# A hybrid decoder trunk on one core: both parts of the input in one 512-column matmul in layer 1

## The chip, the cores and the metric

The kernel runs on one core of a Trainium2 chip. The time is the device time of one execution in microseconds; lower is better. The core has five engines that work side by side and meet through semaphores: PE (TensorE, the matrix multiplier; its weight loads are shown apart as PEld), DVE (VectorE), ACT (ScalarE), POOL (GpSimd) and SP (SyncE, which issues the transfers from the chip's memory). Each engine takes its instructions in the order in which the program wrote them. Matmul results go to PSUM, a memory of eight banks of 512 float32 per partition, and are read from there by ACT or DVE; everything else lies in SBUF.

## The reference

A decoder trunk of two layers, one sequence of 256 tokens behind 16 learned meta tokens, width 2048, all in float32. Layer 0 mixes by attention and a short convolution, layer 1 by a state-space layer (S5) with a gated linear unit behind it; a feed-forward network (FFN) with 5632 hidden channels follows in each.

```python
def s5_mixer(u, ...):
    ...
    g = jax.nn.gelu(y).astype(u.dtype)
    return (g @ w_glu1) * jax.nn.sigmoid(g @ w_glu2)

def swiglu_ffn(h, w_gate, w_up, w_down):
    return (jax.nn.silu(h @ w_gate) * (h @ w_up)) @ w_down

def reference(...):
    h = jnp.concatenate([meta, x], axis=1)
    for i in range(DEPTH):
        u = rms_norm(h, norm_g[i, 0])
        m = attn_conv_mixer(u, ...) if i % 2 == 0 else s5_mixer(u, ...)
        h = h + rms_norm(m, norm_g[i, 1])
        f = swiglu_ffn(rms_norm(h, norm_g[i, 2]), ffn_w_gate[i], ffn_w_up[i], ffn_w_down[i])
        h = h + rms_norm(f, norm_g[i, 3])
    return h[:, N_META:]
```

The change touches `g @ w_glu1`, `g @ w_glu2`, and the products with `w_gate` and `w_up` of layer 1.

## The kernel before

Channels lie on partitions and tokens in the free dimension: an activation is 16 tiles of 128 channels x 272 tokens, in layer 1 from the GLU on 256 (the meta tokens are dropped). A float32 product is made of three matmuls in a faster type (float32r): the weights and the input are each split into a first part and a rest, and hi x xh, hi x xl and lo x xh are added up in PSUM (`mm3`; the fourth product is left out). `xh` and `xl` are the input's parts, `whi` and `wlo` those of the weights.

```python
    def mm3(ps, hi, lo, bh, bl, first, last):
        nc.tensor.matmul(ps, hi, bh, start=first, stop=False)
        nc.tensor.matmul(ps, hi, bl, start=False, stop=False)
        nc.tensor.matmul(ps, lo, bh, start=False, stop=last)
```

Weights come in chunks of two input tiles by up to three output tiles (`Weights`). A chunk is fetched by a DMA issued on SP (`raw`, four buffers), cast on ACT to `whi` (L101), and `raw - whi` is written on DVE as `wlo` (L108). `W.next()`, called ahead of each chunk's matmuls, writes into the program the cast for the chunk two further on and the subtraction for the next one. As the order of an engine is the order of writing, these splits stand on ACT and DVE among whatever else the program writes there at that place. `tick()`, called behind each chunk, writes one piece of queued side work.

The GLU (L1301 on) goes over six blocks of three or two output tiles, 16 chunks each: the second product's and the first's, by turns. After the second product's last chunk (the 14th of the block) ACT takes tanh of each output tile straight from PSUM (L1328); after the first product's last chunk (the 16th) `gate` multiplies on DVE (`tt`, L812) and squares on ACT for the norm. In the first and the last block the gates stand right there, in the others they are queued over the next chunks.

The FFN (`ffn`) goes over thirds of the hidden channels, five blocks of three output tiles each (the very last has two), each block with 16 chunks: gate and up by turns for c = 0 to 7. For c = 0 the matmuls go by part instead of by tile (L755), for c = 1 to 7 `mm3` is called. I number a block's chunks 0 to 15, so 14 is the gate's last and 15 the up's last; 16 and 17 are the first two of what follows. In the last chunks each output tile is multiplied by the norm's factor on DVE on its way out of PSUM (L764 to `gs`, L766 to `us`), and after the gate tiles ACT takes one tanh of all three (L768). Four queued steps then make the hidden activation and its two parts (L774 to L776). A third ends with the down projection, in layer 1 `last_down` (L1379 to L1381), whose moving operand is the weights, 512 columns wide. The first block of each FFN also runs `Sandwich`, which makes the input tiles as the block needs them. A block holds six of the eight PSUM banks, one per output tile and product, of which 256 of 512 columns are used in layer 1.

## Time and profile before

| | us |
|---|---|
| three runs | 2413.26, 2414.88, 2415.72 |
| median | 2414.88 |
| span of the profiled execution (its first to its last instruction) | 2412.0 |

For the profiled execution the span is what is given; it lies 2.9 us under the median of the runs. Of this span the state-space layer ends and the GLU begins at about 1452 us, the GLU ends at 1642, layer 1's FFN runs from there to the end: gate and up blocks to 1826, the first down projection to 1912, and so on by thirds.

In the lines of the profile "L285" is line 285 of the kernel before; `mm<-xh,whi` names what is written and what is read; a shape such as 128x256 is partitions by columns; times in timelines and chains are the start and the length in us, counted from the span's start. A name behind "<-" in square brackets or behind a bar is what ended the idle time before the instruction.

### The profile page before, as it was taken

The page shows a single profiled execution, that of the slowest core. Times are in us where ns is not written, and L with a number is a line of the kernel's source. Part 1 is how long each engine was busy: PE and PEld are TensorE (multiplying, and loading weights), DVE is VectorE, ACT ScalarE, POOL GpSimd, SP SyncE. Part 2 cuts the span into 40 slices and gives each one's busy share as a digit, 9 for nine tenths or more (in the row PEclk, how much of TensorE's full clock was granted, in tenths as well). Part 3 has the DMA queues.
Part 4 walks back from the last instruction along what each step waited for, and adds up shares of the span by engine and source line. Part 5 has one row for each costly group of instructions (what it writes and reads, how often), then busy time and mean ns, then how long its engine had stood idle before and what let it go on. Part 6 is the DMA issues. An engine that isn't in the chain of part 4 may idle for free.

```text
span 2412.0 us, 45528 instructions
## 1 busy us (share of the span) xinstructions
PE 2364.2 (98%) x18038; PEld 2272.2 (94%) x18038; DVE 1437.0 (60%) x2004; ACT 1060.0 (44%) x1613; POOL 705.3 (29%) x1221
## 2 busy tenths in 40 slices
PE   8999999999999999999999889999999999999998
PEld 7999999999999999999999779998998899989996
DVE  6555555686754665656654796457655455645665
ACT  5434434463444343434444555445444444433443
POOL 3000000148775778568501452105000000000001
PEclk9999999999999999999999889999999999999999
DMA  6555555456776777776755864555666566656654
GB/s 171 135 152 142 151 134 181 131 172 182 227 215 208 215 208 215 219 202 200 224 184 166 272 218 157 185 170 155 193 187 206 179 182 179 201 184 186 189 189 155
DMA packets 392537, 447.35 MB, mean 185 GB/s; under 512 B 75476, under 2 KB 324084, under 8 KB 392180
## 3 DMA queue, kind: packets, MB, share of 16 engines
q1 hardware_dynamic: 392096, 444.37, 62.1%
q8 instruction: 141, 2.31, 0.4%
q14 instruction: 72, 0.59, 0.1%
q10 hardware_dynamic: 228, 0.08, 0.0%
HBM read 413.50 MB, written 30.87 MB: 184 GB/s over the span
## 4 chain that ended last, share of the span: by engine, by line
PE 89%; DVE 7%; ACT 1%; DMA 1%; issue 1%; POOL 1%; DVEq 0%; ACTq 0%; SPq 0%; POOLq 0%
PE mm L285 23%; PE mm L287 23%; PE mm L286 23%; PE mm L755 5%; PE mm L1381 3%; PE mm L1380 3%; PE mm L1379 3%; DVE wlo L108 1%; DVE v L1172 1%; DMA raw<-in_ffn_w_gate_dram 1%; PE mm L1030 1%; PE mm L1018 1%; PE aux L483 0%; DVE m L812 0%; DVE rc L812 0%
## 5 line engine op out<-in xcount | busy, mean ns | idle before, releaser
L108 DVE TENSOR_TENSOR wlo<-raw,whi 128x768 fp32r<-128x768 f32 (+2 forms) x891 | 939.7, 1066 | 508.2 <-ACT whi L101 503.7
L101 ACT CAST whi<-raw 128x768 fp32r<-128x768 f32 (+2 forms) x891 | 776.2, 884 | 797.7 <-PE mm L286 496.2
L285 PE MATMUL mm<-xh,whi 128*128 128x272 f32 (+1 forms) x3744 | 1078.0, 288 | 1.0 <-DVE m L812 0.6
L287 PE MATMUL mm<-xh,wlo 128*128 128x272 f32 (+1 forms) x3744 | 1072.8, 287 | 2.7 <-DVE wlo L108 2.1
L286 PE MATMUL mm<-xl,whi 128*128 128x272 f32 (+1 forms) x3744 | 1066.6, 285 | 2.2 <-DVE xl L719 2.1
L287 PEld LDWEIGHTS mm<-xh,wlo 128*128 128x128 f32 x3744 | 707.0, 189 | 6.2 <-DVE wlo L108 6.2
L285 PEld LDWEIGHTS mm<-xh,whi 128*128 128x128 f32 x3744 | 708.6, 189 | 3.6 <-ACT sq L297 0.8
L286 PEld LDWEIGHTS mm<-xl,whi 128*128 128x128 f32 x3744 | 707.3, 189 | 3.2 <-DVE xl L719 3.2
L285 PE MATMUL mm<-ah,whi 128*128 128x272 f32 x960 | 277.6, 289 | 0.5 <-ACT m L678 0.5
L287 PE MATMUL mm<-ah,wlo 128*128 128x272 f32 x960 | 277.0, 289 | 0.0
L286 PE MATMUL mm<-al,whi 128*128 128x272 f32 x960 | 275.7, 287 | 0.0
L812 POOL TENSOR_TENSOR m<-m,gb 128x512 f32<-128x512 f32 x8 | 12.1, 1509 | 711.5 <-ACT mm L1393 695.0
L285 PEld LDWEIGHTS mm<-ah,whi 128*128 128x128 f32 x960 | 180.8, 188 | 1.1 <-ACT m L678 0.7
L286 PEld LDWEIGHTS mm<-al,whi 128*128 128x128 f32 x960 | 180.6, 188 | 0.0
L287 PEld LDWEIGHTS mm<-ah,wlo 128*128 128x128 f32 x960 | 180.3, 188 | 0.1
L302 POOL TENSOR_TENSOR sqacc<-sqacc,sq 128x272 f32<-128x272 f32 (+1 forms) x81 | 83.8, 1035 | 242.9 <-ACT sq L297 241.1
L1380 PE MATMUL mm<-wlo,ah 128*128 128x512 f32 x352 | 137.8, 392 | 1.0 <-DVE wlo L108 1.0
L1379 PE MATMUL mm<-whi,ah 128*128 128x512 f32 x352 | 138.6, 394 | 0.0
L1381 PE MATMUL mm<-whi,al 128*128 128x512 f32 x352 | 138.3, 393 | 0.0
L764 DVE TENSOR_TENSOR gs<-mm,r 128x272 f32<-128x272 f32 (+1 forms) x88 | 38.1, 433 | 113.1 <-PE mm L287 113.1
L580 POOL TENSOR_TENSOR z<-c,x 128x272 f32<-128x272 f32 x8 | 6.3, 792 | 302.7 <-DVE x L573 201.2
L1380 PEld LDWEIGHTS mm<-wlo,ah 128*128 128x128 f32 x352 | 66.2, 188 | 16.3 <-DVE wlo L108 1.7
(408 smaller groups left out, 2509.8 us busy)
## 6 DMA issues: line engine op xcount, KB each, us to landing
raw<-in_ffn_w_gate_dram SPq DMA_DIRECT2D x224, 384.0 KB, 3.8
raw<-in_ffn_w_up_dram SPq DMA_DIRECT2D x224, 384.0 KB, 3.8
raw<-in_ffn_w_down_dram SPq DMA_DIRECT2D x168, 512.0 KB, 4.5
raw<-in_ab_w_in_dram SPq DMA_DIRECT2D x90, 512.0 KB, 4.0
raw<-in_s_w_glu_dram SPq DMA_DIRECT2D x64, 384.0 KB, 3.6
raw<-in_ab_w_o_dram SPq DMA_DIRECT2D x32, 512.0 KB, 4.3
w<-scr SPq DMA_DIRECT2D x16, 768.0 KB, 4.3
scr<-xw SPq DMA_DIRECT2D x16, 512.0 KB, 4.6
```

Source lines behind the costliest of these rows:

```text
L101: self.nc.scalar.copy(hi[:, :n], self.raw[i][:, :n])
L108: self.nc.vector.tensor_tensor(lo[:, :n], raw[:, :n], hi[:, :n].bitcast(F32), op=ALU.subtract)
L285: nc.tensor.matmul(ps, hi, bh, start=first, stop=False)
L286: nc.tensor.matmul(ps, hi, bl, start=False, stop=False)
L287: nc.tensor.matmul(ps, lo, bh, start=False, stop=last)
L302: eng.tensor_tensor(self.acc[:, :self.cols], self.acc[:, :self.cols], sq[:, :self.cols], op=ALU.add)
L755: nc.tensor.matmul(pss[o], w[:, k, o * P:(o + 1) * P], xx[:, k, :cols], start=(k == 0 and w is hi and xx is xh), stop=False)
L764: nc.vector.tensor_tensor(gs[:, o, :cols], pss[o], r["r"][:, :cols], op=ALU.mult)
L1018: nc.tensor.transpose(pt[:, j * P:(j + 1) * P], wide["b"][:, i, j].rearrange("p s h -> p (s h)"), ident)
L1379: nc.tensor.matmul(pss[a], ah[:, kt, ts_], hi[:, k], start=(kt == 0), stop=False)
L1380: nc.tensor.matmul(pss[a], ah[:, kt, ts_], lo[:, k], start=False, stop=False)
L1381: nc.tensor.matmul(pss[a], al[:, kt, ts_], hi[:, k], start=False, stop=(kt == kts - 1))
```

## The change

`xh` and `xl` become the two halves of one tile `xx`, so that one access pattern holds both parts of an input tile. In layer 1's GLU and in layer 1's FFN for c = 1 to 7, `mm2` passes both parts by the same `whi` in one matmul of 512 columns: hi x xh goes to the first half of a PSUM bank and hi x xl to the second; lo x xh then adds to the first half. For c = 0 of the FFN three matmuls remain, of which the one with xl writes the second half. The halves are added later by `both`: ACT copies the second half to SBUF, DVE adds the first. As the norm's factor or the gate no longer comes in the same instruction, POOL multiplies by it in SBUF. In the GLU the second product's tiles are copied, added, and then go through tanh. Layer 0 and the down projections stay.

```diff
-    xh = keep.tile([P, KT, NT], F32R, name="xh")
-    xl = keep.tile([P, KT, NT], F32R, name="xl")
+    xx = keep.tile([P, 2, KT, NT], F32R, name="xx")
+    xh, xl = xx[:, 0], xx[:, 1]
...
+    def mm2(ps, hi, lo, kt):
+        nc.tensor.matmul(ps, hi, xx[:, :, kt, :NREAL], start=(kt == 0), stop=False, skip_group_check=True)
+        nc.tensor.matmul(ps[:, :NREAL], lo, xx[:, 0, kt, :NREAL], start=False, stop=(kt == KT - 1), skip_group_check=True)
+
+    def both(out, ps):
+        nc.scalar.copy(out, ps[:, NREAL:])
+        nc.vector.tensor_tensor(out, out, ps[:, :NREAL], op=ALU.add)
...
     def ffn(m, sw, cols, down=None):
...
-                gps = [bank()[:, :cols] for _ in range(n)]
-                ups = [bank()[:, :cols] for _ in range(n)]
+                halves = cols == NREAL
+                wide_ = 2 * cols if halves else cols
+                gps = [bank()[:, :wide_] for _ in range(n)]
+                ups = [bank()[:, :wide_] for _ in range(n)]
...
                         if c == 0:
                             for k in range(2):
-                                for w, xx in ((hi, xh), (lo, xh), (hi, xl)):
+                                for w, xp in ((hi, xh), (lo, xh), (hi, xl)):
+                                    at = cols if halves and xp is xl else 0
                                     for o in range(n):
-                                        nc.tensor.matmul(pss[o], w[:, k, o * P:(o + 1) * P], xx[:, k, :cols], start=(k == 0 and w is hi and xx is xh), stop=False)
+                                        nc.tensor.matmul(pss[o][:, at:at + cols], w[:, k, o * P:(o + 1) * P], xp[:, k, :cols],
+                                                         start=(k == 0 and w is hi and xp is xh), stop=False, skip_group_check=halves)
...
                         for o in range(n):
                             for k in range(2):
                                 kt = 2 * c + k
-                                mm3(pss[o], hi[:, k, o * P:(o + 1) * P], lo[:, k, o * P:(o + 1) * P],
-                                    xh[:, kt, :cols], xl[:, kt, :cols], False, kt == KT - 1)
-                            if c == 7 and pss is gps:
-                                nc.vector.tensor_tensor(gs[:, o, :cols], pss[o], r["r"][:, :cols], op=ALU.mult)
-                            elif c == 7:
-                                nc.vector.tensor_tensor(us[:, o, :cols], pss[o], r["h"][:, :cols], op=ALU.mult)
+                                w = hi[:, k, o * P:(o + 1) * P], lo[:, k, o * P:(o + 1) * P]
+                                if halves:
+                                    mm2(pss[o], *w, kt)
+                                else:
+                                    mm3(pss[o], *w, xh[:, kt, :cols], xl[:, kt, :cols], False, kt == KT - 1)
+                            if c == 7:
+                                d, rr = (gs, r["r"]) if pss is gps else (us, r["h"])
+                                d, rr = d[:, o, :cols], rr[:, :cols]
+                                if halves:
+                                    both(d, pss[o])
+                                    nc.gpsimd.tensor_tensor(d, d, rr, op=ALU.mult)
+                                else:
+                                    nc.vector.tensor_tensor(d, pss[o], rr, op=ALU.mult)
...
     for a, b in GLU_BLOCKS:
...
         def gate(o, a=a, p1=p1):
-            tt(mr[:, a + o], p1[o], ths[a][:, o], M_)
-            osq.add(mr[:, a + o])
+            t = mr[:, a + o]
+            both(t, p1[o])
+            tt(t, t, ths[a][:, o], M_, G)
+            osq.add(t)
...
-                    mm3((p2, p1)[i][o], hi[:, k, o * P:(o + 1) * P], lo[:, k, o * P:(o + 1) * P],
-                        xh[:, kt, :NREAL], xl[:, kt, :NREAL], kt == 0, kt == KT - 1)
+                    mm2((p2, p1)[i][o], hi[:, k, o * P:(o + 1) * P], lo[:, k, o * P:(o + 1) * P], kt)
...
                 for o in range(n):
-                    nc.scalar.activation(th[:, o], p2[o], AF.Tanh, scale=0.5)
+                    both(th[:, o], p2[o])
+                    nc.scalar.activation(th[:, o], th[:, o], AF.Tanh, scale=0.5)
```

Where a block of layer 1's FFN ends, ACT's rows before are these (first block of the second third; the numbers in names are the weights' chunks, 687 being the next block's first, 688 its second; what an instruction waits for is the engine named in its brackets, DMAHW a transfer):

```order
L101 CAST whi687_22941<-raw687_22873 128x768 [waits DMAHW5_49,DVE_49,PE_49]
L768 ACTIVATE th_22604<-gs_22602 128x3x256 [waits DVE_49]
L101 CAST whi688_22969<-raw688_22897 128x768 [waits DMAHW6_49,PE_49,Activation_49]
L101 CAST whi689_23005<-raw689_22921 128x768 [waits DMAHW7_49,PE_49,Activation_49]
L101 CAST whi690_23030<-raw690_22945 128x768 [waits DMAHW0_49,PE_49,Activation_49]
```

and in the changed kernel

```order
L101 CAST whi687_22060<-raw687_22010 128x768 [waits DMAHW5_49,DVE_49,PE_49]
L297 COPY gs_21793<-mm_21787 128x256 [waits PE_49]
L297 COPY gs_21793<-mm_21788 128x256 [waits PE_49]
L297 COPY gs_21793<-mm_21789 128x256 [waits PE_49]
L790 ACTIVATE th_21795<-gs_21793 128x3x256 [waits Pool_49]
L101 CAST whi688_22088<-raw688_22028 128x768 [waits DMAHW6_49,DVE_49]
L297 COPY us_21794<-mm_21790 128x256 [waits PE_49]
L297 COPY us_21794<-mm_21791 128x256 [waits PE_49]
L297 COPY us_21794<-mm_21792 128x256 [waits PE_49]
L101 CAST whi689_22124<-raw689_22046 128x768 [waits DMAHW7_49,DVE_49]
```

Six copies stand among the casts, and the tanh waits for POOL instead of DVE. DVE's rows at the same place before:

```order
L764 TENSOR_TENSOR gs_22602<-mm_22598,r_20305 128x256 [waits PE_49]
L108 TENSOR_TENSOR wlo687_22971<-raw687_22873,whi687_22941 128x768 [waits DMAHW5_49,Activation_49]
L766 TENSOR_TENSOR us_22603<-mm_22599,rh_20308 128x256 [waits PE_49]
L766 TENSOR_TENSOR us_22603<-mm_22600,rh_20308 128x256 [waits PE_49]
L766 TENSOR_TENSOR us_22603<-mm_22601,rh_20308 128x256 [waits PE_49]
L108 TENSOR_TENSOR wlo688_23007<-raw688_22897,whi688_22969 128x768 [waits DMAHW6_49,DVE_49,Activation_49]
L774 SCALAR_TENSOR_TENSOR gs_22602<-th_22604,gs_22602 128x3x256 [waits DVE_49]
```

and now

```order
L298 TENSOR_TENSOR gs_21793<-gs_21793,mm_21789 128x256 [waits Activation_49]
L108 TENSOR_TENSOR wlo687_22090<-raw687_22010,whi687_22060 128x768 [waits DMAHW5_49,DVE_49]
L298 TENSOR_TENSOR us_21794<-us_21794,mm_21790 128x256 [waits Activation_49]
L298 TENSOR_TENSOR us_21794<-us_21794,mm_21791 128x256 [waits Activation_49]
L298 TENSOR_TENSOR us_21794<-us_21794,mm_21792 128x256 [waits Activation_49]
L108 TENSOR_TENSOR wlo688_22126<-raw688_22028,whi688_22088 128x768 [waits DMAHW6_49,DVE_49]
L796 SCALAR_TENSOR_TENSOR gs_21793<-th_21795,gs_21793 128x3x256 [waits Pool_49]
```

The places on DVE are the same; the multiplies that waited for PE are adds that wait for ACT's copies, and the gate product waits for POOL. In the GLU, after the second product's last chunk of the second block, ACT before had these rows (chunk numbers 494 to 497, 494 being that block's last):

```order
L101 CAST whi494_18280<-raw494_18212 128x768 [waits DMAHW3_49,DVE_49,PE_49]
L1328 ACTIVATE th_18304<-mm_17962 128x256 [waits PE_49]
L1328 ACTIVATE th_18304<-mm_17963 128x256 [waits PE_49]
L1328 ACTIVATE th_18304<-mm_17964 128x256 [waits PE_49]
L101 CAST whi495_18308<-raw495_18236 128x768 [waits DMAHW4_49,DVE_49]
```

and now

```order
L101 CAST whi494_18117<-raw494_18067 128x768 [waits DMAHW3_49,DVE_49,PE_49]
L297 COPY th_18135<-mm_17877 128x256 [waits PE_49]
L1352 ACTIVATE th_18135<-th_18135 128x256 [waits DVE_49]
L297 COPY th_18135<-mm_17878 128x256 [waits PE_49]
L1352 ACTIVATE th_18135<-th_18135 128x256 [waits DVE_49]
L297 COPY th_18135<-mm_17879 128x256 [waits PE_49]
L1352 ACTIVATE th_18135<-th_18135 128x256 [waits DVE_49]
L101 CAST whi495_18145<-raw495_18085 128x768 [waits DMAHW4_49,Activation_49]
```

Between one tile's copy and its tanh ACT now waits for an add on DVE, three times in a row, ahead of the next cast.

More of the change, by code (lines that the diff above doesn't have):

```diff
@@ L1302, in trunk @@
         n = b - a
-        p2 = [bank()[:, :NREAL] for _ in range(n)]
-        p1 = [bank()[:, :NREAL] for _ in range(n)]
+        p2 = [bank() for _ in range(n)]
+        p1 = [bank() for _ in range(n)]
         now = a == 0 or b == KT
```

## The prediction

> **What bounds the kernel now.** I read the page's busy line and chain first, then stretches of layer 1, then the chain and the timeline inside one stretch. On the page TensorE is busy all the time and is most of the chain:
>
> ```profile
> span 2412.0 us, 45528 instructions
> PE 2364.2 (98%) x18038; PEld 2272.2 (94%) x18038; DVE 1437.0 (60%) x2004; ACT 1060.0 (44%) x1613; POOL 705.3 (29%) x1221
> PE 89%; DVE 7%; ACT 1%; DMA 1%; issue 1%; POOL 1%; DVEq 0%; ACTq 0%; SPq 0%; POOLq 0%
> ```
>
> The windows of layer 1 (start:end, length, busy time and count of PE, PEld, DVE, ACT, POOL, granted clock, DMA share, GB/s) are the gated linear unit (GLU) behind its first block, the first block of the FFN, the next four blocks, and the first down projection:
>
> ```profile
> 1490.00:1640.00 150.00, 149.39 (x1258) 149.22 (x1257) 76.04 (x99) 68.19 (x108) 13.30 (x14) 1.00 0.56 181
> 1640.00:1684.00 44.00, 40.06 (x297) 37.68 (x295) 37.46 (x54) 27.83 (x55) 31.33 (x29) 0.92 0.47 137
> 1684.00:1822.00 138.00, 137.37 (x1161) 137.40 (x1162) 79.40 (x102) 60.84 (x76) 0.00 (x0) 1.00 0.64 191
> 1826.00:1908.00 82.00, 82.00 (x376) 67.42 (x375) 39.09 (x37) 38.30 (x48) 0.00 (x0) 1.00 0.62 199
> ```
>
> PE bounds all but the first FFN block, where DVE is the fuller engine (37.46 of 44). In the FFN's blocks POOL does nothing at all. A block's own price comes from the chain (start, length), a 512-column matmul's from the timeline of PE, first and last of 14 rows:
>
> ```profile
> 604.77 4.53 PE mm L755 x36
> 1689.56 4.27 PE mm L755 x36
> ...
> 1723.65 4.27 PE mm L755 x36
> ```
>
> ```profile
> 1889.82 0.39 PE L1379 MATMUL mm<-whi,ah 128*128 128x512 f32 x1
> ...
> 1892.80 0.39 PE L1380 MATMUL mm<-wlo,ah 128*128 128x512 f32 x1
> ```
>
> A block of 288 matmuls of 256 columns takes 1723.65 - 1689.56 = 34.09 us without a gap: 118.4 ns each. Thirteen steps of 512 columns take 2.98 us: 229.2 ns each.
>
> **What it saves.** For each output tile and input tile, three matmuls of 256 columns (355.2 ns) become one of 512 and one of 256 (229.2 + 118.4 = 347.6): 7.6 ns less. The columns streamed stay the same; only one matmul's fixed part goes. There are 16 x 2 x 16 = 512 such triples in the GLU and 44 x 2 x 14 = 1232 in the FFN (its first chunk of each pass keeps three). The first FFN block's 84 give nothing, since DVE sets its pace. 1660 x 7.6 ns = 12.6 us. Bounds, as no row shows two halves 17 KB apart as one moving operand: nothing, if the two halves cost what two matmuls do; and 11.4 ns (18.9 us), if a 256-column matmul behind a 512-column one pays its columns alone (229.2 / 2 = 114.6). I take the rows as they are.
>
> [...]
>
> That fewer weight loads free PE is in the same price: at 272 columns 36 matmuls took 4.53 us against 4.27, so columns, not loads, set the step, and the 512-column rows already hide their load. DMA moves the same bytes. Merging the two parts into one tile changes nothing in layer 0, whose instructions keep their order and waits.
>
> **What it adds.** Each output tile was read out of PSUM by one DVE multiply. Now ACT copies the second half, DVE adds the first, and POOL multiplies (FFN 88 times, GLU gates 16); the GLU's tanh inputs take copy, add, tanh. That is 120 ACT, 16 DVE and 104 POOL instructions more. Their sum is nothing against the idle shares above. What counts is where they stand: ACT and DVE run in order, and behind them stand the weight splits for which PE waits. Here is the end of an FFN block before, chunk 15 (up, c = 7) starting at T = 1755.47, chunk 16 and 17 being the next block's first gate and up chunk:
>
> ```profile
> 1755.35 0.28 PE L287 MATMUL mm<-xh,wlo 128*128 128x256 f32 x1
> 1755.47 0.28 PE L285 MATMUL mm<-xh,whi 128*128 128x256 f32 x1
> ...
> 1759.70 0.53 PE L755 MATMUL mm<-xh,whi 128*128 128x256 f32 x3
> 1760.07 0.52 PE L755 MATMUL mm<-xh,wlo 128*128 128x256 f32 x3
> ```
>
> ```profile
> 1755.67 0.42 DVE L764 TENSOR_TENSOR gs<-mm,r 128x256 f32<-128x256 f32 x1 [0.29 <-PE mm L287]
> 1756.01 0.95 DVE L108 TENSOR_TENSOR wlo<-raw,whi 128x768 fp32r<-128x768 f32 x1
> ...
> 1758.12 0.95 DVE L108 TENSOR_TENSOR wlo<-raw,whi 128x768 fp32r<-128x768 f32 x1
> ```
>
> ```profile
> 1756.12 0.85 ACT L768 ACTIVATE th<-gs 128x768 f32<-128x768 f32 x1 [4.03 <-DVE gs L764]
> 1756.88 2.29 ACT L101 CAST whi<-raw 128x768 fp32r<-128x768 f32 x3
> ```
>
> The second row of wlo is chunk 17's, done at T+3.60; PE asks for it at T+4.60. It has 1.0 us to spare. Prices for the new work (one line's min/median/max ns, then a group with its mean), and from the first FFN block how POOL and DVE fare side by side:
>
> ```profile
> L678 ACT COPY m<-mm x28: 367/385/387, 396.4 to 776.2; 128x272 f32<-128x272 f32 x28
> L1207 POOL TENSOR_TENSOR yq<-yq,yy x16: 723/922/1447, 1375.1 to 1475.7; 128x256 f32<-128x256 f32 x16
> ```
>
> ```profile
> L680 DVE TENSOR_TENSOR m<-m,mm 128x272 f32<-128x272 f32 x32 | 13.3, 437 | 40.0 <-PE mm L287 40.0
> ```
>
> ```profile
> 1656.54 2.90 DVE L108 TENSOR_TENSOR wlo<-raw,whi 128x768 fp32r<-128x768 f32 x2
> 1657.17 1.45 POOL L711 TENSOR_TENSOR hT<-hT,hn 128x256 f32<-128x256 f32 x1
> 1658.59 1.44 POOL L302 TENSOR_TENSOR sqacc<-sqacc,sq 128x256 f32<-128x256 f32 x1
> ```
>
> Alone, a wlo split is 0.95 and a POOL multiply 0.72; side by side both take 1.45. After the change, with 0.03 us per hand-over (1756.09 to 1756.12):
> - gate tiles leave PE at T-1.19, T-0.49 and T+0.20; each is copied (0.38) and added (0.44), and POOL takes them one after the other: from T-0.33, T+0.40 and T+1.13, the last beside chunk 16's wlo (1.4) until T+2.5.
> - tanh, which waits for POOL, starts at T+2.56 and not T+0.65. Behind it on ACT stand chunk 17's whi (0.76 later) and then the three copies of the up tiles (0.76 after that, 0.35 apart): the third ends at T+5.16, its add at T+5.6.
> - chunk 17's wlo stands behind those adds on DVE, beside POOL's up multiplies: T+5.6 + 1.45 = T+7.0.
> - PE asks for it at 2.09 + 2.13 + 0.36 = T+4.58: it waits 2.4 us. Chunk 18's wlo, behind the gate product on DVE (1.4), ends at T+9.3 where PE asks at T+9.1: 0.2 more. Chunk 19's is in time, and the splits catch up at 0.9 us of DVE for 2.1 of PE.
>
> So 2.6 us at each block's end. Where a third ends and the down projection follows, chunk 17 is asked for 0.6 us later, but cast and split are longer: about the same. Fourteen blocks of three tiles x 2.6 + 1.5 for the last of two = 37.9 us. Bounds: without any meeting of POOL and DVE (multiply 0.72, split 0.95) the third up copy ends at T+4.5 and the split at T+5.85: 1.3 us each, 19 in all. If each op shuts the other out for its whole length, splits and multiplies take turns, chunk 17's comes at T+6.9 and chunk 18's at T+10.2: 3.7 each, 54 in all. I take the middle, since the rows show sharing.
>
> In the GLU the second product's tiles go copy, add, tanh three times in a row on ACT, each turn 0.38 + 0.44 + 0.38 and hand-overs, 1.26 us. Counted from chunk 14's start the third add ends at 2.2, chunk 15's wlo behind it at 3.0, and PE asks at 2.3: 0.7 x 6 blocks = 4.2. The first block gates at once, and each gate's square on ACT waits for POOL: a turn of 2.05, the third add at 3.8, chunk 17's wlo at 4.7 against 2.3: 2.4. At the GLU's end nothing covers it:
>
> ```profile
> 1641.48 1.28 ACT L381 ACT_TABLE_LOAD   x1
> 1642.77 0.20 ACT L381 ACTIVATE warm_t<-eps_t 128x1 f32<-128x1 f32 x1
> 1642.88 0.70 ACT L297 ACTIVATE sq<-m 128x256 f32<-128x256 f32 x2
> 1643.33 0.61 PE L314 MATMUL mm<-mean_w,sq 128*128 128x1 f32 x4 [0.91 <-ACT sq L297]
> ```
>
> Two turns of 2.05 from 1642.9 end at 1647.0 where the squares ended at 1643.6: 3.4. The GLU costs 10.0 (bounds 4 to 14). The gates in between are queued over three chunks and stay inside the three chunks' lead of the splits.
>
> **Sum.** -12.6 + 37.9 + 10.0 = +35.3 us on the profiled execution's span of 2412.0, which lies 2.9 under the median of the three runs, 2414.88: 2450.
>
> **Rivals.**
> - *POOL and DVE do not meet* (their turns happen to interleave): 1.3 us per block, -12.6 + 19 + 10 = +16, 2431. For it: a lone POOL multiply is 0.72. Against: in the first FFN block every split beside POOL took 1.45.
> - *They shut each other out whole*: 3.7 per block, -12.6 + 54 + 10 = +51, 2466. The same rows could be read as turns: one split and one POOL op per 1.45 us. [...]
> - *Faster*: the splits' lead of two to three chunks covers the new chain, so only the gain is left: 2414.9 - 12.6 = 2402. It decides at a wait of 0.2 us per block ((12.6 - 10.0) / 15), that is if chunk 17's wlo ends before T+4.8. For it: DVE and ACT are idle 42 and 56% of the four blocks' stretch. Against: even without any meeting I find T+5.85, and what stands between, a tanh, a cast, three copies, three adds, is in order on two engines. If the wait is just about there, 2412.
> - *It does not do what it says*: excluded. The built order has 1744 matmuls fewer and 128x512 ones in their place.
>
> **Chances.** Forecast (sharing, waits of 2 to 3 us) 0.50; no meeting 0.20; whole shut-out 0.15; faster 0.08; about equal 0.07. A difference under 0.2% (4.8 us) can't be told from none here. So faster 0.08, same 0.07, slower 0.85. The lowest case of a slower one is 19 + 4 - 18.9 = +4 (2419), the highest 54 + 14 - 0 = +68 (2483). From 2420 to 2474 leaves out the faster cases and the far end, two in ten.
>
> **What would show it.** Triples of 348 ns in the new two-matmul lines; PE idle by 2 to 3 us at L769 (the block's first chunks) with DVE wlo as releaser, some 14 times; tanh at L790 waiting for POOL; wlo rows of 1.2 to 1.5 us at block ends; PE waiting about 3 us longer for the squares behind the GLU. The forecast is wrong if PE shows no idle at L769 (the cover holds) or if the 512-column matmul from two halves is not 229 ns: at 210 the saving alone would be 45 us.

## The result, and the profile after

| | before | after |
|---|---|---|
| median, us (range) | 2414.89 (2413.26 to 2415.72) | 2476.72 (2473.70 to 2480.05) |
| span of the profiled execution, us | 2412.0 | 2471.8 |

The ratio is put at 1.0267 (95% interval 1.0254 to 1.0279; the two medians alone give 1.0256). By the medians the changed kernel is 61.8 us slower, where +35.3 was forecast, and its 2476.72 lies outside the range given (2420 to 2474). The page of the changed kernel, its span, busy times and chain:

```profile
span 2471.8 us, 42327 instructions
PE 2379.1 (96%) x16294; PEld 2195.3 (89%) x16294; DVE 1458.2 (59%) x2020; ACT 1095.3 (44%) x1733; POOL 818.2 (33%) x1325
PE 79%; DVE 10%; POOL 4%; ACT 3%; issue 2%; DMA 1%; SPq 0%; DVEq 0%; ACTq 0%; POOLq 0%
```

1744 matmuls are gone and PE is busy 15 us longer. On the chain PE's share fell from 89 to 79%, and what came instead is the way from PSUM through DVE, POOL and ACT. By stages of the two traces (places of PE's first and last matmul):

| stage | before, us | after, us | difference |
|---|---|---|---|
| GLU | 190.5 | 203.1 | +12.6 |
| GLU's end to the FFN's first matmul | 6.1 | 10.0 | +3.9 |
| first FFN block | 41.1 | 41.1 | 0 |
| the rest of the FFN | 722.6 | 769.3 | +46.7 |

(The GLU begins 3.3 us earlier than before; its start lies between 1448.3 and 1451.6 in kernels that are alike up to there, so that is no effect of the change. Less these 3.3 the four rows make the 59.8 us by which the two spans differ.)

**The FFN.** What PE waits for in the FFN behind its first block (waiting instruction, what it waited for: total us, times, longest). The view goes from 1700 to 2384 us; before, no wait of PE shows in such a stretch (1685 to 2384):

```profile
PE mm L769 <- DVE wlo L108: 15.3, 12, 1.6
PE mm L1404 <- DVE wlo L108: 4.3, 3, 2.0
PE mm L294 <- DVE wlo L108: 2.5, 4, 0.9
PE mm L769 <- DVE us L298: 2.5, 11, 0.2
```

L769 is the c = 0 chunks of a block (chunk 16 and 17 of the one before). One block's end in the timelines of ACT, DVE, POOL and PE; chunk 15 starts at T = 1737.97:

```profile
1738.17 0.37 ACT L297 COPY gs<-mm 128x256 f32<-128x256 f32 x1 [0.33 <-PE mm L294]
1740.62 0.85 ACT L790 ACTIVATE th<-gs 128x768 f32<-128x768 f32 x1 [2.08 <-POOL gs L786]
1741.37 0.82 ACT L101 CAST whi<-raw 128x768 fp32r<-128x768 f32 x1
1742.09 0.91 ACT L297 COPY us<-mm 128x256 f32<-128x256 f32 x3
```

```profile
1742.49 1.08 DVE L298 TENSOR_TENSOR us<-us,mm 128x256 f32<-128x256 f32 x3 [2.50 <-ACT us L297]
1743.49 1.04 DVE L108 TENSOR_TENSOR wlo<-raw,whi 128x768 fp32r<-128x768 f32 x1
1744.46 1.49 DVE L796 SCALAR_TENSOR_TENSOR gs<-th,gs 128x768 f32<-128x768 f32 x1
1745.87 1.50 DVE L108 TENSOR_TENSOR wlo<-raw,whi 128x768 fp32r<-128x768 f32 x1
```

```profile
1737.74 2.85 POOL L786 TENSOR_TENSOR gs<-gs,r 128x256 f32<-128x256 f32 x3 [27.75 <-DVE gs L298]
1742.99 3.56 POOL L786 TENSOR_TENSOR us<-us,rh 128x256 f32<-128x256 f32 x3 [2.40 <-DVE us L298]
```

```profile
1742.96 0.38 PE L769 MATMUL mm<-xx,whi 128*128 128x256 f32 x1 [0.23 <-DVE us L298]
1744.59 0.62 PE L769 MATMUL mm<-xx,wlo 128*128 128x256 f32 x3 [1.24 <-DVE wlo L108]
...
1746.47 0.39 PE L293 MATMUL mm<-xx,whi 128*128 128x512 f32 x1
```

Read from the top: ACT is idle for 2.08 us until POOL's third product has ended (T+2.62); only then, from T+2.65, come the tanh, the cast of chunk 17, the three up copies; DVE, which had nothing else to do for 2.50 us, adds; and chunk 17's `wlo`, queued behind the adds, is done at T+6.56. From PE's starts (in the second row PE starts 1.63 us behind its last matmul, where a step is 0.12) the block's end costs 0.38 us for a bank that the first up tile still holds, 1.50 for chunk 17's `wlo`, and 0.83 for chunk 18's. Over the whole FFN behind its first block, to the kernel's end, taking each step of PE over 0.45 us less 0.12, such waits make 35.6 us, against 1.2 before.

**A second cost, which the prediction did not have: the clock.** Slices of 3.41 us, laid where the clock's records change (start:end, length, busy time and count of PE, PEld, DVE, ACT, POOL, granted clock, DMA share, GB/s), at one block's end and at two others:

```profile
1740.82:1744.23 3.41, 2.30 (x17) 1.82 (x15) 1.74 (x4) 3.41 (x7) 1.24 (x2) 1.00 0.44 115
1744.23:1747.64 3.41, 2.49 (x17) 2.18 (x18) 3.41 (x4) 0.97 (x2) 2.32 (x2) 1.00 0.38 115
1778.36:1781.78 3.42, 1.95 (x13) 1.47 (x12) 2.75 (x5) 3.39 (x7) 2.24 (x3) 1.00 0.26 93
1781.78:1785.19 3.41, 3.41 (x16) 3.22 (x16) 3.41 (x4) 0.39 (x1) 1.30 (x1) 0.50 0.44 124
1785.19:1788.60 3.41, 3.41 (x21) 3.03 (x20) 3.41 (x5) 2.02 (x3) 0.00 (x0) 1.00 0.74 228
...
2010.45:2013.87 3.42, 1.95 (x14) 1.46 (x12) 2.17 (x5) 3.42 (x8) 1.67 (x2) 1.00 0.33 109
2013.87:2017.28 3.41, 3.41 (x16) 3.41 (x17) 3.41 (x3) 0.54 (x1) 1.88 (x2) 0.50 0.36 115
```

Where both waits of a block's end fall into one slice, PE is busy 1.95 us of it, and in the next slice the clock is 0.50, and 1.00 again in the one behind it. Where the slices cut the waits apart (2.30 and 2.49 us busy), it stays at 1.00. The FFN behind its first block has ten such slices, 10 x 3.41 / 2 = 17.1 us of PE's pace lost; before it has none until its end.

So the FFN's +46.7 is 35.6 - 1.2 of waits, 17.1 of half clock, and a saving of 6.7 (below): 44.8, which leaves 1.9 open. The 17.1 is not all loss, since PE, being slower, reaches the next late `wlo` when it is there: the 0.83 us for chunk 18 shows at none of the eight block ends inside a third that have a half-clock slice. From block end to block end it is 37.26 us with such a slice and 36.55 without, as this part of the chain shows (start and length of the POOL products at successive block ends; a half-clock slice, that of 1781.78, lies between the last two alone):

```profile
1701.19 2.85 POOL gs L786 x3
...
1737.74 2.86 POOL gs L786 x3
...
1774.29 2.86 POOL gs L786 x3
...
1811.55 2.86 POOL gs L786 x3
```

**The GLU.** PE's waits between 1456 and 1651.5 us, then from the GLU's end to the FFN, then in the kernel before at the last two of these places:

```profile
PE mm L294 <- DVE wlo L108: 6.0, 12, 1.3
PE mm L293 <- DVE m L298: 3.9, 1, 3.9
```

```profile
PE mm L325 <- ACT sq L308: 3.8, 2, 3.4
```

```profile
PE mm L285 <- DVE m L812: 0.6, 1, 0.6
PE mm L314 <- ACT sq L297: 0.9, 1, 0.9
```

The wait for the squares at the GLU's end was 0.9 and is 3.4, the one for the first block's gates 0.6 and is 3.9; waits for `wlo` were not there at all. Between two blocks in the middle (ACT, then DVE, then POOL):

```profile
1533.40 0.42 ACT L308 ACTIVATE sq<-m 128x256 f32<-128x256 f32 x1 [2.42 <-POOL m L834]
...
1536.76 0.42 ACT L308 ACTIVATE sq<-m 128x256 f32<-128x256 f32 x1 [1.95 <-POOL m L834]
```

```profile
1531.82 0.95 DVE L108 TENSOR_TENSOR wlo<-raw,whi 128x768 fp32r<-128x768 f32 x1
```

```profile
1531.99 1.38 POOL L834 TENSOR_TENSOR m<-m,th 128x256 f32<-128x256 f32 x1 [34.03 <-DVE m L298]
```

and, for the same product when DVE is idle, a gate of the first block:

```profile
1491.35 0.72 POOL L834 TENSOR_TENSOR m<-m,th 128x256 f32<-128x256 f32 x1 [17.25 <-DVE m L298]
```

Each queued gate holds ACT until POOL has multiplied, and a turn lasts 3.36 us (1533.40 to 1536.76) where PE needs a chunk every 2.1.

### The profile page after: what moved, and what is told of

It is laid out like the page before. It is cut to its first block, busy times and chain, and to the rows that moved or that the text cites. A ratio compares the mean times of both kernels' runs of the same rounds, so it can differ in the third digit from the quotient of the medians.

```text
span 2471.8 us, 42327 instructions
## 1 busy us (share of the span) xinstructions
PE 2379.1 (96%) x16294; PEld 2195.3 (89%) x16294; DVE 1458.2 (59%) x2020; ACT 1095.3 (44%) x1733; POOL 818.2 (33%) x1325
## 4 chain that ended last, share of the span: by engine, by line
PE 79%; DVE 10%; POOL 4%; ACT 3%; issue 2%; DMA 1%; SPq 0%; DVEq 0%; ACTq 0%; POOLq 0%
PE mm L286 14%; PE mm L288 14%; PE mm L287 14%; PE mm L293 13%; PE mm L294 7%; PE mm L769 3%; PE mm L1404 3%; PE mm L1405 3%; PE mm L1403 3%; DVE wlo L108 3%; POOL gs L786 2%; DVE v L1194 1%; ACT whi L101 1%; POOL m L834 1%; PE mm L1052 1%
## 5 line engine op out<-in xcount | busy, mean ns | idle before, releaser
L293 PE MATMUL mm<-xx,whi 128*128 128x512 f32 x1744 | 617.8, 396 | 4.6 <-DVE m L298 3.9
L286 PE MATMUL mm<-xx,whi 128*128 128x272 f32 x2000 | 586.0, 293 | 0.4 <-ACT whi L101 0.4
L288 PE MATMUL mm<-xx,wlo 128*128 128x272 f32 x2000 | 581.2, 291 | 2.6 <-DVE wlo L108 2.4
L287 PE MATMUL mm<-xx,whi 128*128 128x272 f32 x2000 | 577.2, 289 | 1.8 <-DVE xx L730 1.7
L294 PE MATMUL mm<-xx,wlo 128*128 128x256 f32 x1744 | 492.5, 282 | 8.8 <-DVE wlo L108 8.5
L293 PEld LDWEIGHTS mm<-xx,whi 128*128 128x128 f32 x1744 | 331.0, 190 | 81.2 <-DVE m L298 4.2
L288 PEld LDWEIGHTS mm<-xx,wlo 128*128 128x128 f32 x2000 | 378.1, 189 | 4.5 <-DVE wlo L108 4.5
L287 PEld LDWEIGHTS mm<-xx,whi 128*128 128x128 f32 x2000 | 379.0, 189 | 2.7 <-DVE xx L730 2.7
L286 PEld LDWEIGHTS mm<-xx,whi 128*128 128x128 f32 x2000 | 378.2, 189 | 2.4 <-ACT whi L101 0.8
L294 PEld LDWEIGHTS mm<-xx,wlo 128*128 128x128 f32 x1744 | 329.8, 189 | 16.5 <-DVE wlo L108 16.0
L786 POOL TENSOR_TENSOR gs<-gs,r 128x256 f32<-128x256 f32 x44 | 42.5, 994 | 560.6 <-DVE gs L298 560.6
```

Source lines behind the costliest of these rows:

```text
L293: nc.tensor.matmul(ps, hi, xx[:, :, kt, :NREAL], start=(kt == 0), stop=False, skip_group_check=True)
L294: nc.tensor.matmul(ps[:, :NREAL], lo, xx[:, 0, kt, :NREAL], start=False, stop=(kt == KT - 1), skip_group_check=True)
L786: nc.gpsimd.tensor_tensor(d, d, rr, op=ALU.mult)
```

## The experiments

Ratios, and differences given as such, are to the kernel before, run beside each kernel (its median lay between 2411.43 and 2412.32; beside the changed kernel 2414.89). All changes are to the changed kernel unless said otherwise. In the code "..." stands for lines left out.

**The matmul alone.** The output tile is read from the first half, as before; hi x xl is computed but not added in the GLU and in the gate and up products.

```diff
-                                    both(d, pss[o])
-                                    nc.gpsimd.tensor_tensor(d, d, rr, op=ALU.mult)
+                                    nc.vector.tensor_tensor(d, pss[o][:, :cols], rr, op=ALU.mult)
...
-            both(t, p1[o])
-            tt(t, t, ths[a][:, o], M_, G)
+            tt(t, p1[o][:, :NREAL], ths[a][:, o], M_)
...
-                    both(th[:, o], p2[o])
-                    nc.scalar.activation(th[:, o], th[:, o], AF.Tanh, scale=0.5)
+                    nc.scalar.activation(th[:, o], p2[o][:, :NREAL], AF.Tanh, scale=0.5)
```

> The matmuls of the change alone: 512 + 256 columns as in the change, but each output tile is read out of PSUM by one DVE multiply (GLU: one ACT tanh, one DVE multiply) as before, from the first half only, so the product of the weights' first part with the input's second part is left out of layer 1's GLU and gate and up products. Theory 1 (the loss is all in the way the tiles leave PSUM): PE never waits at block ends, and 1660 triples save 7.6 ns each by the prediction, 12.6 us, so 2402; by the changed kernel's own steps (232.2 + 120.2 against 357.1 ns, 4.7 ns) 7.8 us, so 2407. Rival (the matmul over two halves 17 KB apart is itself the loss): 2425 or more, with triples over 357 ns.

Measured: 2401.83 us against 2411.43, ratio 0.9958 (0.9945 to 0.9970), 9.6 us faster. The chain of this kernel, one block's first chunk and the next one's:

```profile
1717.64 4.28 PE mm L769 x36
...
1751.24 4.27 PE mm L769 x36
```

A block takes 33.60 us in place of 34.09: 0.49 / 84 = 5.8 ns a triple, and 1660 x 5.8 = 9.6. The gain is real, and smaller than the 12.6 of the forecast. The rival, a loss in the matmul itself, is out: PE waits for no `wlo` at a block's end here.

**The evacuation alone.** Three matmuls of 256 columns again, the one with xl into the second half; copies, adds and POOL products as in the change.

```diff
-        nc.tensor.matmul(ps, hi, xx[:, :, kt, :NREAL], start=(kt == 0), stop=False, ...)
+        nc.tensor.matmul(ps[:, :NREAL], hi, xh[:, kt, :NREAL], start=(kt == 0), stop=False, ...)
+        nc.tensor.matmul(ps[:, NREAL:], hi, xl[:, kt, :NREAL], start=False, stop=False, ...)
```

> The other part alone: three matmuls of 256 columns as before, the product with the input's second part going into the bank's second half, and the tiles leaving PSUM as in the change (ACT copy, DVE add, POOL multiply). Theory 1: the change's time plus the saving that is given up, 2477 + 8 = 2485, with the same waits at block ends. If the saving is the predicted 7.6 ns a triple: 2489. Rival (the matmul is the loss): below 2440.

Measured: 2481.00, ratio 1.0289 (1.0273 to 1.0305), +69.6 us, near theory 1 (2485) and far above the rival's 2440. PE's waits in the FFN repeat those of the change (all lines one further down):

```profile
PE mm L770 <- DVE wlo L108: 15.3, 12, 1.6
```

-9.6 + 69.6 = +60.0 against +61.8 for both together: the two parts add up, and the whole loss lies in the way out of PSUM.

**The tanh later.** In the FFN the tanh is written behind the up copies instead of ahead of them; nothing else.

```diff
-                        if c == 7 and pss is gps:
+                        if c == 7 and pss is (ups if halves else gps):
                             nc.scalar.activation(th[:, :n, :cols], gs[:, :n, :cols], AF.Tanh, scale=0.5)
```

> The change with one instruction moved: in layer 1's FFN the gate tiles' tanh on ACT is written behind the up tiles' copies instead of ahead of the next chunk's cast. Work, engines and transfers are the same. Theory 1 (chunk 17's split comes late because its cast and the up copies stand behind a tanh that waits for POOL): the waits of 1.5 us at 14 block ends go, and with them the stretches at half clock; 3.1 us per block end for 14 or 15 ends, 43 to 46 us less: 2431 to 2434. Rival (POOL and DVE shutting each other out is what makes the splits late, wherever the tanh stands): at most 1 us per block less, 2462 or more.

Measured: 2428.93, ratio 1.0073 (1.0059 to 1.0087), 2 us under theory 1's range and far from the rival's 2462. One instruction, moved on one engine, brings back some 44 us with every added instruction still there (61.8 less 17.5, each against the kernel before beside it; in the traces the FFN behind its first block takes 725.0 in place of 769.3). What is left of PE's waits in its FFN:

```profile
PE mm L294 <- DVE wlo L108: 3.5, 12, 0.5
PE mm L1404 <- DVE wlo L108: 1.6, 2, 1.0
```

and no slice at half clock is left in the FFN behind its first block. That shows the cause of the FFN's loss: the tanh, which waits for POOL, stood ahead of the cast and the copies in ACT's queue.

**Work in the wait.** 13 more matmuls of 256 columns, whose result is overwritten, ahead of the up pass of twelve FFN blocks; they fill PE's wait for chunk 17.

```diff
+                            if halves and pss is ups and a > t0:
+                                for f in range(13):
+                                    nc.tensor.matmul(ups[0][:, :cols], held[:, 0, :P], xh[:, 0, :cols], start=True, stop=True, ...)
+                            held = hi
```

> The change with 13 matmuls of 256 columns more ahead of the up pass of 12 FFN blocks of layer 1 (a block's first up chunk, where PE waits for its split), whose results are overwritten: 156 matmuls x 118 ns = 18.5 us of PE work put into the waits. Theory 1 with the clock (PE idle for 1.5 us sets the clock to half for 3.4 us behind most of these waits): the stretches at clock 0.5 at those places go, and the time is the same or less although there is more work: the blocks with a dip take 37.26 us and those without 36.55, so 8 x 0.7 = 6 us less, 2471. Rival (the dips cost nothing of their own, being a sign of the wait): the same time, 2477, if the wait just covers the work, and up to 18 us more if it doesn't.

Measured: 2469.23, ratio 1.0237 (1.0223 to 1.0251), +57.8 us where the change has +61.8, although PE does 156 x 118.4 ns = 18.5 us more. In the traces the FFN behind its first block takes 762.2 us in place of 769.3, 7.1 less. Its slices behind the same block's end:

```profile
1780.00:1784.00 4.00, 3.68 (x31) 3.47 (x30) 2.75 (x5) 3.96 (x8) 2.25 (x3) 1.00 0.26 94
1784.00:1788.00 4.00, 3.45 (x23) 2.94 (x23) 4.00 (x5) 0.97 (x2) 1.31 (x1) 1.00 0.40 125
```

The granted clock is 1.00 where the change has 0.50. Counted as above, waits and half clock fall from 35.6 and 17.1 to 25.6 and 1.7 us: 25.4 less, and 18.5 of added work make 6.9. It is thus shown that here the clock fell for PE's idleness, and that the fall is worth about 7 us net in the FFN. The block ends say the same: eight of the ten slices lie inside a third, 8 x (37.26 - 36.55) = 5.7, and of the other two, at down projections, one is gone with the added work and one is not.

**The GLU's order as well.** The late tanh, and in the GLU all copies and adds of a block ahead of its tanhs, a gate's square one tick behind its product.

```diff
                 for o in range(n):
                     both(th[:, o], p2[o])
+                for o in range(n):
                     nc.scalar.activation(th[:, o], th[:, o], AF.Tanh, scale=0.5)
...
-            queues[0].extend([[lambda o=o, g=gate: g(o)] for o in range(n)])
+            gs_, qs_ = [lambda o=o, g=gate: g(o) for o in range(n)], [lambda o=o, g=square: g(o) for o in range(n)]
+            queues[0].extend([[f] for f in gs_[:2]] + [gs_[2:3] + qs_[:1]] + [[f] for f in qs_[1:]])
```

> The changed kernel with three moves in the order of the instructions and nothing else: the FFN's tanh stands behind the up copies (as in e3_late_tanh), in the GLU the two or three copies and adds of a block come before its tanhs, and a gate's square stands one tick behind its product (behind all products in the first and last block). Theory A (what is lost in the GLU too is order: ScalarE waits in its queue for GpSimd's product or VectorE's add, and the weight parts behind it come late): ScalarE's waits of 2.4 us for m of GpSimd go, TensorE's 24 waits of 1.3 us for wlo lose those of the GLU, the wait of 3.4 us for sq at the GLU's end shrinks by about 2 us; from 2428.9 of e3 down to 2412-2419. Rival B (the GLU loses because VectorE has an add, a product's neighbour and slower weight parts more per block, whatever the order): it stays at 2425-2430.

Measured: 2417.09, ratio 1.0018 (1.0009 to 1.0028), within theory A. PE's waits in the GLU:

```profile
PE mm L293 <- DVE m L298: 0.9, 1, 0.9
PE mm L294 <- DVE wlo L108: 0.6, 1, 0.6
```

6.0 and 3.9 us became 0.6 and 0.9, and the GLU takes 189.1 us where it took 190.5 before and 203.1 with the change. One part of the expectation missed: the wait of 3.4 us for the squares at the GLU's end stayed, since there the squares wait for copy, add and product whatever stands between.

**VectorE in POOL's place.** The order of the change, both products on DVE.

```diff
-                                    nc.gpsimd.tensor_tensor(d, d, rr, op=ALU.mult)
+                                    nc.vector.tensor_tensor(d, d, rr, op=ALU.mult)
...
-            tt(t, t, ths[a][:, o], M_, G)
+            tt(t, t, ths[a][:, o], M_)
```

> The changed kernel with the product by the scale (FFN) and by the gate (GLU) on VectorE in place of GpSimd; the order of the instructions is the change's. Theory A (the FFN loses because the tanh waits in ScalarE's queue for the last product, and GpSimd's products take 0.99 us each in a row): VectorE's product of 256 columns takes some 0.35 to 0.4 us as its add does (0.42), the tanh starts about 1.3 us earlier, and the wait of 1.5 us for chunk 17's wlo shrinks to about 0.2-0.9 us a block, with fewer places at half clock; 2476 less 14 x 1.0 to 1.5 and less 3 to 8 in the GLU, 2445-2460. Rival B (the order alone decides, the engine does not, since any chain of copy, add and product ahead of the tanh makes the weight parts late, and VectorE has 3 x 0.4 us more of its own in front of them): within 5 us of the changed kernel, 2470-2480. Rival C (GpSimd's sharing with VectorE is the whole cost): as e3, 2425-2435.

Measured: 2468.50, ratio 1.0228 (1.0213 to 1.0243): 1.5 us under the range of rival B, and further from those of A and C. DVE at a block's end:

```profile
1735.16 0.42 DVE L786 TENSOR_TENSOR gs<-gs,r 128x256 f32<-128x256 f32 x1
1735.50 0.95 DVE L108 TENSOR_TENSOR wlo<-raw,whi 128x768 fp32r<-128x768 f32 x1
1737.49 0.42 DVE L298 TENSOR_TENSOR us<-us,mm 128x256 f32<-128x256 f32 x1 [1.03 <-ACT us L297]
...
1739.53 0.42 DVE L786 TENSOR_TENSOR us<-us,rh 128x256 f32<-128x256 f32 x1
1739.87 0.95 DVE L108 TENSOR_TENSOR wlo<-raw,whi 128x768 fp32r<-128x768 f32 x1
```

```profile
PE mm L769 <- DVE wlo L108: 25.2, 13, 2.5
```

No instruction is slowed by POOL here: each split is 0.95, each product 0.42. The tanh starts earlier (1.70 us behind chunk 15's start in place of 2.65), but now three products stand among the adds in front of chunk 17's `wlo`, and PE waits up to 2.5 us for it. The FFN behind its first block takes 770.4 us, as long as with the change (769.3); what is gained lies in the GLU (198.1 for 203.1). So the FFN loses as much with no POOL in it, and with the late tanh it loses little with POOL in it: the meeting of POOL and DVE is not what cost the time, the chain in front of the split is.

**Stage by stage.** The late tanh with the GLU as before, and the changed GLU with the FFN as before.

```diff
-                    mm2((p2, p1)[i][o], hi[:, k, o * P:(o + 1) * P], lo[:, k, o * P:(o + 1) * P], kt)
+                    mm3((p2, p1)[i][o], hi[:, k, o * P:(o + 1) * P], lo[:, k, o * P:(o + 1) * P],
+                        xh[:, kt, :NREAL], xl[:, kt, :NREAL], kt == 0, kt == KT - 1)
...
```

(The gate and the tanhs of the GLU, not shown, are those of the kernel before too.)

> The FFN of e3_late_tanh (the change with the tanh behind the up copies), and the GLU as in the kernel before: three matmuls, one VectorE product out of PSUM, one tanh out of PSUM. Theory A (the parts add up by stage): e3's FFN from its first full block to the end took 725.0 us against 722.6 before, so 2411.4 + 2.4 = 2414 (2411-2416), with the waits of 0.65 us for wlo behind each block's chunk 16 still there: the saving of 0.49 us a block is given back there. Rival B (e3's waits in the FFN were set off by the later, shifted start of the stream in the GLU): they go, and the time is 2403-2407.

```diff
-                halves = cols == NREAL
+                halves = False
```

> The GLU of the change (matmul of 512 columns, copy, add, product on GpSimd), and the FFN of layer 1 as in the kernel before. Theory A (the GLU costs what its stage shows): the changed kernel's first FFN block began 13.1 us later than before's (1702.53 against 1689.40), and the FFN then takes its 722.6: 2411.4 + 13 = 2424 (2421-2428). Rival B (part of the 13 us is the clock at half speed behind the long wait at 1495 and behind the GLU's end, which comes and goes): 2415-2421. Rival C (the GLU's delay leaves the weight stream ahead and the FFN catches up): 2410-2415.

Measured: 2414.10, ratio 1.0009 (1.0000 to 1.0018), theory A; and 2427.24, ratio 1.0060 (1.0043 to 1.0077), theory A, +15.1 us. The GLU's loss is its own, and the FFN's is 61.8 - 15.1 = 46.7, as the stages showed.

**The gate's product a chunk later.** In the kernel with the late tanh and the old GLU, PE still waited up to 0.5 us for chunk 18's `wlo`, with the gate's product (L796) ahead of it on DVE. An empty tick is queued in front of it within a third.

```diff
-                queues[2].extend([
+                queues[2].extend([[]] * (b < t1) + [
```

> e7_late_ffn_only with one move more: within a third of the FFN the gate's product (VectorE, 0.95 us alone and 1.49 beside GpSimd) is queued one chunk later, so that it stands behind chunk 17's and 18's weight parts. Theory A (the last wait of 0.65 us behind each block's 36 first matmuls is this product standing in front of a wlo): the rows of PE mm L294 waiting for wlo in the FFN vanish, the block falls from 34.12 to 33.5 us, and the time from 2414.1 by 12 x 0.5 to 0.65, to 2406-2409; this would be below the kernel before (2412.1). Rival B (the splits then fall behind at the next instruction, since VectorE has more work per block than before): the wait moves by a chunk or two, and the time stays within 2 us of 2414.

> e5_late_all with the same move of the gate's product by one chunk. Theory A: 2417.1 less 6 to 8, 2409-2411; the GLU's part of it is still some 2 to 3 us dearer than in e9_ffn_blank (the squares at its end). Rival B: stays at 2415-2418.

Measured: 2407.69, ratio 0.9984 (0.9975 to 0.9993), and with the changed GLU 2410.23, ratio 0.9992 (0.9983 to 1.0001): theory A in both. The first kernel's chain:

```profile
1720.49 4.27 PE mm L769 x36
...
1754.09 4.28 PE mm L769 x36
```

33.60 us a block, that of the matmul alone: within a third the longer way out of PSUM now costs nothing at a block's end. The FFN behind its first block takes 719.2 us against 716.2 with the matmul alone, so some 3 us are still lost, most of them behind the start of the last block.

**The halves 1 KB apart.** The matmul alone, the tile laid out so that an input tile's two parts are neighbours.

```diff
-    xx = keep.tile([P, 2, KT, NT], F32R, name="xx")
-    xh, xl = xx[:, 0], xx[:, 1]
+    xx = keep.tile([P, KT, 2, NT], F32R, name="xx")
+    xh, xl = xx[:, :, 0], xx[:, :, 1]
...
```

> e1_matmul_alone (the matmul of the change, the product with the input's second part not read, evacuation as before) with the two halves of the moving operand 1 KB apart and not 17 KB (tile laid out channel tile by channel tile). Theory A (a triple saves 5.8 and not 7.6 ns because the two halves lie far apart): the 512-column matmul falls from 232.1 to about 229.2 ns, as with one run of columns, 1660 x 1.8 to 2.9 ns = 3 to 5 us, 2397-2399. Rival B (the distance is free, and the 232 ns belong to the switch from 256 to 512 columns and back): 232 ns again, 2401-2403.

Measured: 2400.58, ratio 0.9953 (0.9939 to 0.9967), not to be told from 0.9958. The time lies between the ranges of the two theories, so the chain has to tell them apart:

```profile
1714.85 4.24 PE mm L769 x36
1748.48 4.24 PE mm L769 x36
```

33.63 us a block against 33.60, and the 512-column matmul's step is 232 to 233 ns in both: the distance costs nothing, theory A is out. (That the switch of widths causes the 232 ns is not shown by this.)

**The change where it has cover.** The kernel with the empty tick, the changed GLU only in its four middle blocks.

```diff
+        wide_ = NREAL if now else 2 * NREAL
...
+                    if now:
+                        mm3(*w, xh[:, kt, :NREAL], xl[:, kt, :NREAL], kt == 0, kt == KT - 1)
+                    else:
+                        mm2(*w, kt)
```

> e9_ffn_blank, and in the GLU the change for the four blocks in the middle alone (11 of 16 output tiles), with the order of e10_all_blank (copies and adds before the tanhs, squares a tick later); its first and last block stay as before. Theory A (the matmul pays where the longer evacuation has cover, and the GLU's first and last block have none): 352 triples x 4.7 to 6 ns = 1.7 to 2.1 us under e9_ffn_blank's 2407.7, 2405-2407, with the wait of 3.3 us for sq at the GLU's end back at 0.9. Rival B (the middle blocks' copies and adds still delay weight parts): at or above 2407.7, with waits at L294 inside the GLU.

Measured: 2406.72, ratio 0.9979 (0.9969 to 0.9989), theory A by its time, though its difference to the 2407.69 of the kernel with the empty tick is too small to be told. Nor does the trace bear it out: the GLU takes 190.3 us against 190.5, where theory A has 1.7 to 2.1 less. That the matmul pays in the four middle blocks is thus not shown. It and the kernel with the empty tick are 4 to 6 us faster than the kernel before, with intervals that leave out 1.

## Why the prediction was wrong, point by point

Of the sum's terms, -12.6 for the matmuls came to -9.6, +37.9 for the FFN's block ends to +53.4 (46.7 and the saving of 6.7), and +10.0 for the GLU to +18.1. Two steps failed. The sum let a wait of PE cost its own length, with no term for the clock behind it (17.1 us gross in the FFN, some 7 net), and it put the GLU's queued gates at nothing (5.3 us of late splits). The points below take these apart.

- **Sign and mechanism: right.** Slower, because POOL's product holds the tanh, the tanh holds the copies on ACT, and the splits on DVE come late for L769. Moving the tanh alone showed it in the FFN.
- **The saving: mis-sized.** 7.6 ns a triple was taken from 229.2 and 118.4 ns of rows at equal widths; alternating, the starts lie some 232 and 119 apart in the kernel with the matmul alone. By the block's period (less its first chunk, over 84) a triple takes some 349 ns against 355; the period's own 0.49 us are 5.8 ns each, 9.6 us in all, not 12.6. Inside the bounds given (0 to 18.9).
- **Waits at a block's end: near in sum, partly by luck.** 37.9 us forecast, 35.6 measured in the FFN, against 1.2 before. The chain up to the adds came out within 0.15 us: tanh at T+2.65 for T+2.56, third up copy at T+5.03 for T+5.16, adds done at T+5.6. Then chunk 17's `wlo` took 1.04 and not 1.45, and PE came 0.4 later, held by a PSUM bank that the forecast had not looked at: 1.50 in place of 2.4. Chunk 18 cost 0.83 in place of 0.2 where the clock stayed full, and nothing where it fell; without the fall the waits would have come to more. A block end at full clock costs 2.95 us (36.55 against the 33.60 of the matmul alone), where 2.6 was forecast.
- **The clock: missing.** This is the largest step that failed in the FFN: the sum took waits to cost their own length. Ten times in the FFN a slice of 3.41 us in which PE idled for 1.89 us or more was followed by one at half clock: 17.1 us gross there, some 7 net, and 1.7 gross in the GLU. A row quoted in the prediction had shown it (a granted clock of 0.92 in the stretch with the first FFN block, 44 us of which 40 busy), and it was not asked why. The same row was read as DVE being the fuller engine, with 37.46 us; PE's own 40.06 stand beside it. (That this block gives nothing came out so: 41.1 us in both.)
- **FFN in all:** forecast 37.9 - 1148 x 0.0076 = +29.2, measured +46.7. The gap of 17.5 is, gross, 17.1 (clock), -2.3 - 1.2 (waits), 2.0 (saving: 8.7 forecast, 6.7), and 1.9 that stays open.
- **GLU: +6.1 forecast (10.0 - 3.9), +15.1 measured.** "The gates in between stay inside the lead" failed: six late splits behind queued gates make 5.3 us by PE's steps, since a gate's turn takes 3.36 us and a chunk 2.1. The tanh inputs' waits came as forecast (six steps of 0.78 to 0.85, 0.66 to 0.73 each over the usual 0.12, for 0.7: 4.2 in all). The first block's end cost 3.9 and not 2.4, and not for chunk 17's `wlo` but for the bank that its third gate's add set free. At the GLU's end it was 2.4 (a step of 3.63 for 1.19) in place of 3.4. With 1.7 of half clock and 1.3 in two steps at the GLU's start (where PE still waits for the state-space layer), less a saving of 512 x 5.8 ns = 3.0, this makes 4.2 + 5.3 + 3.3 + 2.4 + 1.7 + 1.3 - 3.0 = 15.2 (the first block's end counted as 3.3, a step of 4.16 for 0.89).
- **The rivals.** Whole shut-out gave 2466, the nearest, for waits of 3.7 us a block. That is luck: it had chunk 17's and 18's `wlo` done at T+6.9 and T+10.2, the forecast at T+7.0 and T+9.3, and the rows above have T+6.56 and T+9.40. The GLU's rows speak for its reading at least in part (last section). But it was not the cause: without POOL's products the loss stayed at 2.3%. "No meeting" was priced at 1.3 us a block with a fast POOL; in the kernel with no meeting the block's end cost more (25.2 us of waits at L769, in 13 places), though there the products took DVE's own time, which is not that rival's case.

## What to carry to other kernels

Before instructions are added on an idle engine, write down the order of each in-order queue at that place and ask what waits ahead of the work that the bound engine needs next; an instruction that waits for a slow engine (here the tanh, for POOL's three products of 2.85 us) belongs behind that work, and moving this one tanh was worth 44 of 62 us. Price a new wait of the matrix engine with the clock that it may cost behind it (in the FFN here 17.1 us gross, some 7 net). The gain of 9.6 us in the matmuls was only had here once the longer way out of PSUM was taken off the weights' path; then it was 4 to 6 us.

## What the runs showed of the hardware

- **In the trace of the change the clock goes by slices of 3.41 us on a fixed grid.** In its FFN the half-clock slices start whole multiples of 3.41 us apart (1781.78 and 2013.87 above: 68 slices). PE's idle time in the slice before, worked out from its starts, was 1.89 us or more in all ten. The slices followed by full clock had 1.56 us or less, but for two with 1.91 and 2.00 (at the edge of a down projection and at the last block). So in this trace up to 1.56 us of idle time in 3.41 was followed by full clock, and 1.89 or more by half clock but for these two: the bound is not sharp.
- **POOL and DVE at the same time.** In the GLU of the change a split that began 0.17 us before POOL's product kept its 0.95 us, and the product took 1.38 where POOL alone takes 0.72. So the later one bore the whole delay there, 0.66 us; that both get slower side by side, as the prediction read the rows, is not what these rows show. At an FFN block's end, where products and splits follow each other, both engines' rows are long (`wlo` 1.50, three products 3.56); they do not tell turns from a slowing of both.
- **A 512-column matmul between 256-column ones:** in the two kernels with the matmul alone the next one starts some 232 ns later, whether the 512 columns' two halves lie 17 or 1 KB apart.
